# Four gate groups of a hybrid decoder layer as a seven-product block, with its operand sums kept in memory

## The chip, the cores and the metric

The kernel runs on one core of a Trainium2 chip. The metric is the device time of one execution in microseconds (us). The kernel before takes 2213.79 us, the median of 3 runs (2211.71 to 2217.8).

## What is computed

One layer on 1024 tokens with a width of 1024. From the normalised input h come three branches (an mLSTM, a causal differential attention, a cross-attention into 256 memory tokens). Each is projected, multiplied by a sigmoid gate made from h, and summed; an output projection, a residual and an MLP follow. What the change touches is the gate:

```
h     = RMSNorm(x)                                  # 1024 x 1024
gates = sigmoid(h @ w_gate + b_gate)                # 1024 x 3072: 1024 columns for each branch
merged = sum over the branches b of  gates[b] * (y[b] @ w_proj[b])
x = x + merged @ w_out
x = x + relu(RMSNorm(x) @ w_up)**2 @ w_down
```

All of it is float32. TensorE gets each operand as two parts, a rounded high part and the rest (`split`, L104 to L112: ScalarE casts, VectorE subtracts), and a product takes three matmuls, high with high, high with low and low with high (`mm3`).

## The kernel before

`hT` holds h, transposed and split, in SBUF: 8 slices k of 128 features, each with a high and a low part of 1024 tokens. `gate_steps` (L446) is a generator that makes the gates in 12 groups of 256 columns. A group is four products of 128 columns with 512 tokens, and each sums over the 8 slices: 4 x 8 x 3 = 96 matmuls of 128x512. ScalarE takes each product out of PSUM with a tanh (tile `gt`, L471), and SyncE (SP) stores it to `gates` in memory (L472). The 16 weight tiles of 256 KB and their splits (`gate_load`, L431) come two slices at a time.

The order of the work is that of the program text, spread over the engines by a scheduler; where `self.pinned` is set, TensorE's order is that of the text. The table `(2, 1, 1, 2, 6)` cuts the 12 groups into runs: two beside the cross-attention, one and one inside the mLSTM branch, two behind it (the loop at `pg`), and a last run of six, of which three serve as filling inside the attention (until `gdone` is 288) and three follow it (`pgh`).

`branch_d` is the differential attention. Its `d_gemm` (L907) makes 64 tiles of 128 tokens with 384 columns (q, k and v of half a head), 24 matmuls each. A tile is called d tile here. ScalarE copies a d tile's q and k to `draw` (L947), squares them into `dscr` (L949), casts v to `dv` (L111); VectorE sums the squares (L953) and makes the low part of v (L112). Only then is the PSUM bank free. All of these products, gates too, share two banks in turn (`mm_tile`, `kmm` = 2), so a product can start when the last but one has been taken out. Weight tiles `raw` from `in_wd` come by SP and are split into `w` (128x384).

The last instructions of the mLSTM branch are two ScalarE scalings of `ym` (L771), and SP stores each to y (L327). `ym` has one buffer, so the second waits until the first store has landed.

`tail` (L1274) projects and merges. `k_tiles` (L1262) loads a branch's y in 8 tiles `kraw` of 512 KB through two buffers and splits them into `kt`; the first group of 256 columns takes them in that order, 12 matmuls to a tile. The third branch's y comes first.

Of the kernel before, what the change touches and what calls it, by code (L numbers as in the profile page):

```python
# [10 lines left out]
F32 = mybir.dt.float32  # L11
F32R = mybir.dt.float32r
AF = mybir.ActivationFunctionType
# [4 lines left out]
P = 128  # L18
# [3 lines left out]
NK = 8  # L22
# [9 lines left out]
def f32(ap):  # L32
    return ap.bitcast(F32)
# [38 lines left out]
class Layer:  # L72
# [359 lines left out]
    def gate_load(self, pool=None):  # L432

        pool = pool or self.gwp
        n = self.gate_n
        if n == 12 * NK:
            return
# [528 lines left out]
    def branch_d(self, pool):  # L966
# [649 lines left out]
    def run(self):  # L1616
        tc, nc = self.tc, self.nc
        with ExitStack() as ctx:
# [21 lines left out]
            self.rd = dt("r_d", (16, P, 7, 512))  # L1640
            with ExitStack() as c1:
# [6 lines left out]
                with ExitStack() as c2:  # L1648
# [10 lines left out]
                    self.gates = self.gate_steps((2, 1, 1, 2, 6))  # L1659
# [19 lines left out]
                with tc.tile_pool(name="wpg", bufs=13, reuse_waits="tile") as self.wp, tc.tile_pool(name="rpg", bufs=3, reuse_waits="tile") as self.rp:  # L1679
                    self.gwp, self.grp = self.wp, self.rp  # L1680
                    with tc.tile_pool(name="pg", bufs=2) as self.gpool:
                        for _ in range(2 * 32):
                            next(self.gates)
                    cg.close()
                    with tc.tile_pool(name="pd", bufs=2) as pd, tc.tile_pool(name="pd3", bufs=3) as pd3, tc.tile_pool(name="pdm", bufs=1) as pdm, tc.tile_pool(name="pd5", bufs=7) as pd5, tc.tile_pool(name="pdv", bufs=5) as pdv, tc.tile_pool(name="pdv2", bufs=17) as pdv2, tc.tile_pool(name="pd4", bufs=4) as pd4:
# [6 lines left out]
                        class T4:  # L1692
                            def tile(_, shape, dt, tag, name):
                                tag = "dscr2" if tag == "gt" else tag
                                p = pd5 if tag == "draw" else pdv if tag == "drr" else pdv2 if tag == "dv" else pd4 if tag in ("dk", "dkl") else pdm if tag == "dpe1" else pd3 if tag in ("daT", "dst") else pdm if tag in ("dscr", "dscr2", "y", "dsg") else pd
# [12 lines left out]
def pack(i):  # L1708
# [28 lines left out]
    w["wgate"] = np.stack([grp(wg, r(256 * g, 256)) for g in range(12)])  # L1737
# [33 lines left out]
```

## Time and profile before

| | before |
|---|---|
| time, median of 3 runs | 2213.79 us |
| the profiled execution | 2213.57 us, its span 2211.8 us |
| TensorE matmuls busy | 2163.4 us, 98% |
| VectorE, ScalarE, GpSimd busy | 62%, 44%, 24% |
| bytes moved by DMA | 273.06 MB, mean 123 GB/s |

The span is the time between the first and the last recorded instruction, and 1.8 us of the execution lie around it. TensorE is busy nearly all the time, but its ends are modelled, so this says that it rarely waits and not that it runs at its peak. In the rows, PE is TensorE, DVE is VectorE, ACT is ScalarE, POOL is GpSimd, and SPq is the queue of transfers that SP issues. L91 and L94 are the helpers through which every matmul and transpose goes, L111 and L112 the two halves of `split`, so such groups are told apart by their tiles.

### The profile page before, as it was taken

To read this page: it belongs to the slowest core of one execution; us is meant where nothing else is said; L and a number is where in the kernel's file an instruction comes from. 1 tells how busy PE (TensorE), PEld (TensorE's weight loads), DVE (VectorE), ACT (ScalarE), POOL (GpSimd) and SP (SyncE) were. 2 spreads that over 40 slices of the span, in tenths; PEclk is the share of its full clock that TensorE was granted. 3 is DMA by queue.
4 is the path that set the end of the run, shared out by engine and by line. 5 is a ranking of instruction groups with operands and counts; after the bars stand their busy time and mean duration, and the time that the engine had idled before them with its cause. 6 is when DMAs were issued, how large, how long until landed. Compare 5 with 4: busy or idle time off the path is not lost.

```text
span 2211.8 us, 30588 instructions
## 1 busy us (share of the span) xinstructions
PE 2163.4 (98%) x11097; PEld 1860.7 (84%) x11097; DVE 1361.4 (62%) x2598; ACT 980.7 (44%) x1962; POOL 527.8 (24%) x696
## 2 busy tenths in 40 slices
PE   7999999999999999999999999999999999899999
PEld 5878888898899999999888888877787888688887
DVE  6643575565237777777641232544688877767779
ACT  6543355454336666666542120223444444543332
POOL 2100000000011111111000003202557655565553
PEclk9999999999999999999999999999999999999999
DMA  7023122121333333333343443436435444854444
GB/s 250 29 81 115 50 91 76 44 82 39 107 109 86 93 84 84 88 92 86 101 148 114 134 142 126 138 110 205 147 115 198 159 147 147 318 196 146 145 145 170
DMA packets 127948, 273.06 MB, mean 123 GB/s; under 512 B 12945, under 2 KB 21430, under 8 KB 125750
## 3 DMA queue, kind: packets, MB, share of 16 engines
q1 hardware_dynamic: 125494, 258.53, 37.2%
q10 hardware_dynamic: 2304, 12.58, 1.4%
q8 instruction: 87, 1.43, 0.3%
q14 instruction: 63, 0.52, 0.1%
HBM read 178.76 MB, written 67.14 MB: 111 GB/s over the span
## 4 chain that ended last, share of the span: by engine, by line
PE 77%; DVE 9%; DMA 6%; ACT 4%; issue 2%; POOL 2%; SPq 0%; DVEq 0%; ACTq 0%; POOLq 0%
PE mm L91 46%; PE p L91 20%; PE sc L91 6%; PE tp L94 2%; PE po L91 2%; DVE acc L67 1%; DMA kraw<-y 1%; DMA xr<-h_d 1%; DVE wo L67 1%; DMA y<-yd 1%; DVE u L67 1%; DVE w L112 1%; DMA wraw<-in_wup 0%; DVE xts L67 0%; DVE c L67 0%
## 5 line engine op out<-in xcount | busy, mean ns | idle before, releaser
L91 PE MATMUL mm<-w,hT 128*128 128x384 f32 (+3 forms) x2496 | 473.4, 332 | 8.3 <-DVE dsg L112 5.4
L91 PE MATMUL mm<-hT,w 128*128 128x512 f32 x1920 | 465.7, 395 | 0.0
L91 PEld LDWEIGHTS mm<-hT,w 128*128 128x128 f32 x1920 | 353.5, 188 | 74.2
L91 PEld LDWEIGHTS mm<-w,hT 128*128 128x128 f32 x2496 | 389.2, 190 | 22.2 <-DVE dsg L112 7.6
L91 PE MATMUL p<-xd,wo 128*128 128x512 f32 x1344 | 310.0, 393 | 5.7 <-DVE c L67 2.2
L91 PE MATMUL p<-xo,wo 128*128 128x512 f32 x1344 | 308.2, 390 | 5.7 <-DVE st L1418 2.6
L91 PEld LDWEIGHTS p<-xd,wo 128*128 128x128 f32 x1344 | 253.8, 189 | 61.7 <-DVE c L67 3.3
L91 PEld LDWEIGHTS p<-xo,wo 128*128 128x128 f32 x1344 | 251.0, 188 | 61.5 <-DVE u L67 3.7
L91 PE MATMUL mm<-kt,w 128*128 128x512 f32 x1152 | 262.2, 389 | 1.9 <-ACT w L111 1.1
L112 DVE TENSOR_TENSOR w<-raw,w 128x256 fp32r<-128x256 f32 (+3 forms) x304 | 173.0, 590 | 137.9 <-ACT w L111 136.8
L91 PEld LDWEIGHTS mm<-kt,w 128*128 128x128 f32 x1152 | 216.0, 188 | 47.9 <-ACT w L111 1.5
L111 ACT CAST w<-raw 128x256 fp32r<-128x256 f32 (+3 forms) x304 | 154.3, 530 | 178.9 <-PE mm L91 114.5
L104 ACT CAST wo<-wraw 128x896 fp32r<-128x896 f32 x122 | 115.0, 945 | 208.9 <-PE p L91 115.2
L67 DVE TENSOR_TENSOR wo<-wraw,wo 128x896 fp32r<-128x896 f32 x122 | 143.7, 1195 | 59.4 <-ACT wo L104 59.4
L1145 POOL TENSOR_TENSOR wraw<-wraw 128x128 f32<-128x128 f32 x128 | 97.3, 760 | 245.8 <-DMA wraw<-in_wdown 108.1
L1007 ACT ACTIVATE dpe<-sc,dst,drr 128x256 f32<-128x256 f32 (+7 forms) x128 | 106.7, 834 | 99.7 <-DVE dst L1003 92.0
L999 DVE CUSTOM_DVE_ANT_0 sc<-sc,tmask 128x256 f32<-128x256 f32 (+7 forms) x128 | 97.0, 758 | 12.6 <-PE sc L91 12.5
L127 POOL TENSOR_SCALAR hss<-hss 128x4 f32<-128x4 f32 x8 | 3.3, 410 | 415.4 <-ACT mscr L752 272.9
L91 PE MATMUL sc<-dk,dq 128*128 128x512 f32 (+3 forms) x384 | 90.4, 343 | 0.0
L1148 POOL TENSOR_TENSOR wraw<-wraw 128x128 f32<-128x128 f32 x128 | 85.6, 669 | 10.0
L1146 POOL TENSOR_TENSOR wraw<-wraw 128x128 f32<-128x128 f32 x128 | 87.3, 682 | 0.0
L1147 POOL TENSOR_TENSOR wraw<-wraw 128x128 f32<-128x128 f32 x128 | 87.2, 682 | 0.0
(283 smaller groups left out, 2832.6 us busy)
## 6 DMA issues: line engine op xcount, KB each, us to landing
dk<-dsg SPq DMA_DIRECT2D x64, 256.0 KB, 4.4
wraw<-in_wup SPq DMA_DIRECT2D x64, 256.0 KB, 3.4
r_d<-xts SPq DMA_DIRECT2D x16, 1024.0 KB, 4.1
wraw<-in_wdown SPq DMA_DIRECT2D x64, 256.0 KB, 3.1
xd<-r_d SPq DMA_DIRECT2D x19, 768.0 KB, 7.4
xd<-r_d SPq DMA_DIRECT2D x14, 1024.0 KB, 6.8
raw<-in_wgate SPq DMA_DIRECT2D x48, 256.0 KB, 3.2
gates<-gt SPq DMA_DIRECT2D x48, 256.0 KB, 2.0
```

The lines of the kernel that those rows point to most:

```text
L67: return self.tc.keep_in_program_order(f(*a, **k))
L91: self.pin(self.nc.tensor.matmul(out, l, r, start=start, stop=stop))
L94: self.pin(self.nc.tensor.transpose(out, x, self.ident))
L104: self.A.copy(hi, src)
L111: nc.scalar.copy(hi, src)
L112: nc.vector.tensor_sub(lo, src, f32(hi))
L999: V.tensor_tensor_reduce(out=sc[:, 0:n], in0=sc[:, 0:n], in1=self.tmask[:, D - n : D], scale=1.0, scalar=-3.0e38, op0=ALU.add, op1=ALU.max ...
L1007: nc.scalar.activation(pe[c][:, 0:n], sc[:, 0:n], AF.Exp, bias=t8[:, 2 + c : 3 + c], scale=rr[:, i, c : c + 1], accum_out=t8[:, 4 + c : 5 ...
L1145: G.tensor_add(r[:, 4], r[:, 0], r[:, 3])
L1146: G.tensor_sub(r[:, 5], r[:, 4], r[:, 1])
L1147: G.tensor_sub(r[:, 6], r[:, 1], r[:, 0])
L1148: G.tensor_sub(r[:, 7], r[:, 2], r[:, 5])
```

## The change

Groups 8 to 11 are taken out of the generator, which now has runs of (2, 1, 1, 1, 3): one group follows the mLSTM branch where two did, and the attention is filled with three as before. A new function `wino_gates` makes the other four behind the attention. It takes 256 features by 256 columns as a 2 x 2 block of operands, and gets the four quarter products from seven products in place of eight, by the table `PROD`: for each of 4 units (256 columns), 7 products over 4 slice pairs, 3 matmuls each, 84 in place of 96. VectorE and ScalarE add the products up (`u2`, `c11`, `u3`, `c21`). Five of the seven need sums of operands. Those of the weights are made by GpSimd as the tiles come in (32 operations of 128x256). Those of h are four sets of 2 MB; `h_sums` makes them beside the one group that is left behind the mLSTM branch, for each of 4 slice pairs one VectorE addition of 128x2048 (`hb`), three VectorE subtractions and one GpSimd subtraction of 128x512 (`ht`), and a split of 128x2048 (`ho`), stores them to `hc_d`, and `wino_gates` loads four tiles `hx` of 2 MB. In the attention some tiles have pools of their own. The weights of the last four groups are packed as quarters (`wgq`, 256 KB a tile as before).

```diff
--- before.py
+++ after.py
@@ -433,7 +433,7 @@
 
         pool = pool or self.gwp
         n = self.gate_n
-        if n == 12 * NK:
+        if n == 8 * NK:
             return
         g, k = divmod(n, NK)
         if k % 2 == 0:
@@ -1110,9 +1110,112 @@
                 combine(s)
         fill(8)
         norm(15, 2)
-        assert self.gdone <= 288
-        while self.gdone < 288:
+        assert self.gdone <= 256
+        while self.gdone < 256:
             next(gates)
+        self.pinned = False
+
+    def h_sums(self, pool, op):
+
+        nc, V, G = self.nc, self.nc.vector, self.nc.gpsimd
+        for kp in range(4):
+            b = pool.tile([P, 4, 512], F32, tag="hb", name=self.name("hb"))
+            t = pool.tile([P, 4, 512], F32, tag="ht", name=self.name("ht"))
+            o = op.tile([P, 4, 2, 512], F32R, tag="ho", name=self.name("ho"))
+            h = f32(self.hT[:, 2 * kp : 2 * kp + 2])
+            V.tensor_add(b.rearrange("p (k h) n -> p k (h n)", k=2), h[:, :, 0], h[:, :, 1])
+            V.tensor_sub(t[:, 0], b[:, 0], b[:, 1])
+            G.tensor_sub(t[:, 2], b[:, 2], b[:, 0])
+            V.tensor_sub(t[:, 1], b[:, 2], t[:, 0])
+            V.tensor_sub(t[:, 3], b[:, 3], t[:, 1])
+            self.split(o[:, :, 0], o[:, :, 1], t)
+            nc.sync.dma_start(
+                self.hcd[:, :, kp].rearrange("q p n -> p q n"), f32(o).rearrange("p q a n -> p q (a n)")
+            )
+
+    def wino_gates(self, base):
+
+        nc, V, A, G = self.nc, self.nc.vector, self.nc.scalar, self.nc.gpsimd
+        one = lambda name, bufs=1: base.enter_context(tc.tile_pool(name=name, bufs=bufs, reuse_waits="tile"))
+        tc = self.tc
+        gtp, ev, x3, x6, rr, x5, x4 = one("fgt", 2), one("fev", 2), one("fx3"), one("fx6"), one("fr", 3), one("fx5"), one("fx4")
+        X = {}
+        for q, p in ((4, x4), (5, x5), (6, x6), (3, x3)):
+            X[q] = p.tile([P, 4, 2, 512], F32R, tag="x", name=self.name("hx"))
+        raws, W = {}, []
+
+        def load(n):
+            if n < 8:
+                u, kk = divmod(n, 2)
+                r = rr.tile([P, 8, 2, P], F32, tag="fr", name=self.name("fr"))
+                for i in range(2):
+                    nc.sync.dma_start(r[:, 0:4, i], self.a["wgq"][u][:, 2 * kk + i])
+                G.tensor_add(r[:, 4], r[:, 0], r[:, 3])
+                G.tensor_sub(r[:, 5], r[:, 4], r[:, 1])
+                G.tensor_sub(r[:, 6], r[:, 1], r[:, 0])
+                G.tensor_sub(r[:, 7], r[:, 2], r[:, 5])
+                raws[n] = r
+
+        def wsp():
+            n = len(W)
+            if n < 56:
+                u, r = divmod(n, 14)
+                j, kk = divmod(r, 2)
+                t = self.wp.tile([P, 2, 256], F32R, tag="w", name=self.name("w"))
+                self.split(t[:, 0], t[:, 1], raws[2 * u + kk][:, 1 + self.PROD[j][0]].rearrange("p k n -> p (k n)"))
+                W.append(t)
+                if j == 6:
+                    load(2 * u + 3 + kk)
+
+        def x_(q, kp, i):
+            if q >= 3:
+                return X[q][:, kp, i]
+            k, hf = divmod(q + 1, 2)
+            return self.hT[:, 2 * kp + k, i, hf * 512 : hf * 512 + 512]
+
+        for n in range(3):
+            load(n)
+        for q in (4, 5, 6, 3):
+            nc.sync.dma_start(f32(X[q]).rearrange("p k a n -> p k (a n)"), self.hcd[q - 3])
+        for _ in range(9):
+            wsp()
+        self.pinned = True
+        tl = lambda n: ev.tile([P, 512], F32, tag=n, name=self.name(n))
+        for u in range(4):
+            def out(i, c):
+                ft, s = 16 + u * 2 + i // 2, slice(i % 2 * 512, i % 2 * 512 + 512)
+                t = gtp.tile([P, 512], F32, tag="gt", name=self.name("gt"))
+                A.activation(t, c, AF.Tanh, bias=self.bg[:, ft : ft + 1], scale=0.5)
+                nc.sync.dma_start(self.gdr[ft, :, s], t)
+
+            for j, (l, q) in enumerate(self.PROD):
+                ps = self.mm_tile()
+                for kp in range(4):
+                    w = W[u * 14 + 2 * j + kp // 2]
+                    c = slice(kp % 2 * P, kp % 2 * P + P)
+                    self.mm3(ps, (w[:, 0, c], w[:, 1, c]), (x_(q, kp, 0), x_(q, kp, 1)), kp == 0, kp == 3)
+                    if kp % 2:
+                        wsp()
+                if j == 0:
+                    u2, c11, u3, c21 = (tl(n) for n in ("u2", "c11", "u3", "c21"))
+                    A.copy(u2, ps)
+                elif j == 1:
+                    V.tensor_add(c11, u2, ps)
+                    out(1, c11)
+                elif j == 2:
+                    V.tensor_add(u2, u2, ps)
+                elif j == 3:
+                    V.tensor_add(u3, u2, ps)
+                elif j == 4:
+                    V.tensor_add(c21, u3, ps)
+                    out(3, c21)
+                elif j == 5:
+                    V.tensor_add(u3, u3, ps)
+                    V.tensor_add(u2, u2, ps)
+                    out(2, u3)
+                else:
+                    V.tensor_add(u2, u2, ps)
+                    out(0, u2)
@@ -1638,6 +1741,7 @@
             self.x1d = dt("x1_d", (8, P, D))
             self.h2d = dt("h2_d", (8, P, D))
             self.rd = dt("r_d", (16, P, 7, 512))
+            self.hcd = dt("hc_d", (4, P, 4, 1024))
             with ExitStack() as c1:
                 E1 = lambda *x, **k: c1.enter_context(tc.tile_pool(*x, **k))
                 self.pmm = E1(name="pmm", bufs=1, space=PSUM)
@@ -1656,7 +1760,7 @@
                                 p = tmp8 if tag == "xk" else tmp if tag in ("mx", "sq", "r1", "r4") else tmp0
                                 return p.tile(shape, dt, tag=tag, name=name)
                         self.phase_x(kv, T())
-                    self.gates = self.gate_steps((2, 1, 1, 2, 6))
+                    self.gates = self.gate_steps((2, 1, 1, 1, 3))
                     with tc.tile_pool(name="pc", bufs=2) as pc, tc.tile_pool(name="pc1", bufs=1) as pc1, tc.tile_pool(name="pc3", bufs=5) as pc3, tc.tile_pool(name="pc4", bufs=6) as pc4, tc.tile_pool(name="wpc", bufs=8) as self.gwp, tc.tile_pool(name="rpc", bufs=2) as self.grp:
                         class T2:
                             def tile(_, shape, dt, tag, name):
@@ -1678,11 +1782,15 @@
                     self.branch_m(T3(), gm, 1, gnext)
                 with tc.tile_pool(name="wpg", bufs=13, reuse_waits="tile") as self.wp, tc.tile_pool(name="rpg", bufs=3, reuse_waits="tile") as self.rp:
                     self.gwp, self.grp = self.wp, self.rp
-                    with tc.tile_pool(name="pg", bufs=2) as self.gpool:
-                        for _ in range(2 * 32):
+                    with tc.tile_pool(name="pg", bufs=2) as self.gpool, tc.tile_pool(name="phs", bufs=1, side="right", reuse_waits="tile") as phs, tc.tile_pool(name="pho", bufs=2, side="right", reuse_waits="tile") as pho:
+                        self.h_sums(phs, pho)
+                        for _ in range(32):
                             next(self.gates)
                     cg.close()
...
                         self.gpool = T4()
                         self.branch_d(T4())
-                    with tc.tile_pool(name="pgh", bufs=2) as self.gpool:
-                        for _ in self.gates:
-                            pass
+                    with ExitStack() as c3:
+                        self.wino_gates(c3)
             self.tail()
```

On VectorE the end of the mLSTM branch and the start of the attention read so before. `w` are weight splits (`raw` 128x384 for the d tiles), and the last rows take out d tile 0 (`mm_6090`, `dv_6119`) and d tile 1.

```order
L112 TENSOR_TENSOR w_6343<-raw_6280,w_6343 128x384
L112 TENSOR_TENSOR w_6354<-raw_6282,w_6354 128x384
L112 TENSOR_TENSOR w_6363<-raw_6282,w_6363 128x384
L112 TENSOR_TENSOR w_6381<-raw_6284,w_6381 128x384
L953 TENSOR_REDUCE drr_6089<-dscr_6117 128x4
L112 TENSOR_TENSOR dv_6119<-mm_6090,dv_6119 128x128
L953 TENSOR_REDUCE drr_6089<-dscr_6150 128x4
```

And so in the changed kernel, the last of the four sets and the same d tile (`mm_6007`, `dv_6036`):

```order
L112 TENSOR_TENSOR w_6298<-raw_6201,w_6298 128x384
L1126 TENSOR_TENSOR hb_5812<-hT 128x2048
L112 TENSOR_TENSOR ho_5803<-ht_5802,ho_5803 128x4x512
L1127 TENSOR_TENSOR ht_5813<-hb_5812 128x512
L1129 TENSOR_TENSOR ht_5813<-hb_5812,ht_5813 128x512
L1130 TENSOR_TENSOR ht_5813<-hb_5812,ht_5813 128x512
L112 TENSOR_TENSOR ho_5814<-ht_5813,ho_5814 128x4x512
L953 TENSOR_REDUCE drr_6006<-dscr_6034 128x4
L112 TENSOR_TENSOR dv_6036<-mm_6007,dv_6036 128x128
```

All four sets stand ahead of the two VectorE operations that free the bank of d tile 0. From the first `hb`, which stands behind two weight splits, to `dv_6036` there are 4 `hb`, 12 `ht`, 4 `ho`, 11 weight splits, and the last two rows. On ScalarE the cast of the last `ho` stands in the same way ahead of the copy of d tile 0.

At the start of the tail SP issues the loads of the third branch's y (`kraw`) so before; `in_wpc` are weights of the projection, and the weights of the last gate groups are loaded behind these rows:

```order
L472 DMA gates<-gt_12188 128x512
L327 DMA y<-yd_12200 128x512
L1268 DMA kraw_12913<-y 128x1024
L1268 DMA kraw_12918<-y 128x1024
L137 DMA raw_12953<-in_wpc 128x1024
L472 DMA gates<-gt_12265 128x512
```

And so in the changed kernel, where `gt_12915`, `gt_12963`, `gt_12981` and `gt_12998` are the four outputs of the last unit:

```order
L1189 DMA gates<-gt_12915 128x512
L137 DMA raw_13283<-in_wpc 128x1024
L1371 DMA kraw_13117<-y 128x1024
L1189 DMA gates<-gt_12963 128x512
L1371 DMA kraw_13122<-y 128x1024
L1189 DMA gates<-gt_12981 128x512
L1408 DMA gl_13267<-gates 128x512
L1408 DMA gl_13271<-gates 128x512
L1189 DMA gates<-gt_12998 128x512
L1371 DMA kraw_13127<-y 128x1024
```

The first load of y has moved from the start of the last three groups to the last unit of the block: its buffer takes memory of the operand tile `hx` that the fifth product of a unit reads, and it waits for that product's last matmul in the fourth unit, two products (24 matmuls) before the end of the block. The second load stands behind the store of the output `gt_12963`, and the third behind that of the last output.

## Rows read from the trace of the kernel before

**Rows 1.** The page, first lines: span, and TensorE's busy time.

```profile
span 2211.8 us, 30588 instructions
PE 2163.4 (98%) x11097; PEld 1860.7 (84%) x11097; DVE 1361.4 (62%) x2598; ACT 980.7 (44%) x1962; POOL 527.8 (24%) x696
```

**Rows 2.** TensorE's waits: line and tile, releaser, us in total, times, longest.

```profile
PE mm L91 <- DVE dsg L112: 5.4, 7, 0.9
...
PE mm L91 <- DVE w L112: 3.8, 3, 3.0
```

**Rows 3.** Timeline, gates and tail: start, us, engine, line, out<-in, xcount [idle before].

```profile
1151.72 66.94 PE L91 MATMUL mm<-hT,w 128*128 128x512 f32 x294
1218.50 43.68 PE L91 MATMUL mm<-kt,w 128*128 128x512 f32 x192
```

**Rows 4.** Timeline, end of the mLSTM branch, two groups, first d tiles.

```profile
575.53 44.40 PE L91 MATMUL mm<-hT,w 128*128 128x512 f32 x192
576.10 0.73 ACT L771 ACTIVATE ym<-tho,dv 128x512 f32<-128x512 f32 x1 [0.42 <-DVE tho L768]
...
576.93 0.40 SPq L327 DMA_DIRECT2D y<-ym  x1
...
615.76 3.28 DVE L112 TENSOR_TENSOR w<-raw,w 128x384 fp32r<-128x384 f32 x5 [24.00 <-ACT w L111]
...
619.77 19.43 PE L91 MATMUL mm<-w,hT 128*128 128x384 f32 x111
```

**Rows 5.** Tiles `xts` and `xo` (MLP operands): ns min/median/max, first and last start.

```profile
L1127 DVE TENSOR_TENSOR xts<-xr x4: 692/693/962, 1523.4 to 1593.0; 128x512 f32<-128x512 f32 x4
L1128 POOL TENSOR_TENSOR xts<-xr x4: 1383/1742/1797, 1523.5 to 1591.2; 128x512 f32<-128x512 f32 x4
L1129 DVE TENSOR_TENSOR xts<-xr,xts x4: 680/1667/1672, 1524.1 to 1594.3; 128x512 f32<-128x512 f32 x4
...
L111 ACT CAST xo<-xts x4: 1891/1916/1919, 1526.6 to 1596.3; 128x2048 fp32r<-128x2048 f32 x4
L112 DVE TENSOR_TENSOR xo<-xts,xo x4: 2278/2429/2586, 1528.7 to 1599.1; 128x2048 fp32r<-128x2048 f32 x4
```

**Rows 6.** Groups by line and shape: busy us, mean ns, then idle before.

```profile
L112 DVE TENSOR_TENSOR w<-raw,w 128x384 fp32r<-128x384 f32 x64 | 34.6, 554 | 32.4 <-ACT w L111 31.4
...
L953 DVE TENSOR_REDUCE drr<-dscr 128x4 f32<-128x256 f32 x64 | 26.5, 415 | 30.0 <-ACT dscr L949 30.0
...
L112 DVE TENSOR_TENSOR dv<-mm,dv 128x128 fp32r<-128x128 f32 x64 | 18.1, 283 | 0.1
```

**Rows 7.** DMA issues: tensors, count, KB each, median us to landing.

```profile
r_d<-xts SPq DMA_DIRECT2D x16, 1024.0 KB, 4.1
...
kraw<-y SPq DMA_DIRECT2D x24, 512.0 KB, 4.5
...
y<-ym SPq DMA_DIRECT2D x16, 256.0 KB, 2.0
```

**Rows 8.** Timeline of TensorE around its waits behind `w`, `st`.

```profile
1533.26 1.22 PE L91 MATMUL mm<-mh,w 128*128 128x512 f32 x2 [3.00 <-DVE w L112]
...
1589.32 7.05 PE L91 MATMUL p<-xo,wo 128*128 128x512 f32 x30 [2.62 <-DVE st L1418]
```

**Rows 9.** Stretches: us, busy by engine, then granted TensorE clock, DMA share, GB/s.

```profile
202.00:208.00 6.00, 5.27 (x21) 4.89 (x22) 2.83 (x8) 3.08 (x9) 0.00 (x0) 0.50 0.42 132
...
1533.00:1536.00 3.00, 2.74 (x7) 2.17 (x8) 2.42 (x2) 0.00 (x0) 1.33 (x1) 0.50 0.80 181
...
1589.00:1592.00 3.00, 2.68 (x12) 2.27 (x13) 1.86 (x4) 3.00 (x6) 2.65 (x3) 1.00 0.32 93
```

**Rows 10.** Tile `kraw` (ns min/median/max), then us from issue to landing.

```profile
L111 ACT CAST kt<-kraw x24: 1047/1052/1057, 1160.5 to 1409.7; 128x1024 fp32r<-128x1024 f32 x24
L112 DVE TENSOR_TENSOR kt<-kraw,kt x24: 1210/1225/1433, 1161.6 to 1410.7; 128x1024 fp32r<-128x1024 f32 x24
...
DMA to landing us min/median/max: 3.2/4.5/6.7
```

More of the change, by code (lines that the diff above doesn't have):

```diff
@@ L1680, in run @@
                     self.gwp, self.grp = self.wp, self.rp
-                    with tc.tile_pool(name="pg", bufs=2) as self.gpool:
-                        for _ in range(2 * 32):
+                    with tc.tile_pool(name="pg", bufs=2) as self.gpool, tc.tile_pool(name="phs", bufs=1, side="right", reuse_waits="tile") as phs, tc.tile_pool(name="pho", bufs=2, side="right", reuse_waits="tile") as pho:
+                        self.h_sums(phs, pho)
+                        for _ in range(32):
                             next(self.gates)
                     cg.close()
-                    with tc.tile_pool(name="pd", bufs=2) as pd, tc.tile_pool(name="pd3", bufs=3) as pd3, tc.tile_pool(name="pdm", bufs=1) as pdm, tc.tile_pool(name="pd5", bufs=7) as pd5, tc.tile_pool(name="pdv", bufs=5) as pdv, tc.tile_pool(name="pdv2", bufs=17) as pdv2, tc.tile_pool(name="pd4", bufs=4) as pd4:
+                    with ExitStack() as c3:
+                        E3 = lambda name, bufs: c3.enter_context(tc.tile_pool(name=name, bufs=bufs, reuse_waits="tile"))
+                        pdo, pdy, pdv2, pdm, pds, pd5 = E3("pdo", 2), E3("pdy", 1), E3("pdv2", 17), E3("pdm", 1), E3("pds", 1), E3("pd5", 7)
+                        pdv, pd, pd3, pd4 = E3("pdv", 5), E3("pd", 2), E3("pd3", 3), E3("pd4", 4)
                         self.tmask = pdm.tile([P, D], F32, name="tmask")
@@ L1694, in tile @@
                                 tag = "dscr2" if tag == "gt" else tag
-                                p = pd5 if tag == "draw" else pdv if tag == "drr" else pdv2 if tag == "dv" else pd4 if tag in ("dk", "dkl") else pdm if tag == "dpe1" else pd3 if tag in ("daT", "dst") else pdm if tag in ("dscr", "dscr2", "y", "dsg") else pd
+                                p = {
+                                    "draw": pd5, "drr": pdv, "dv": pdv2, "dk": pd4, "dpe1": pdm, "daT": pd3, "dst": pd3,
+                                    "dscr": pds, "dsg": pds, "dscr2": pdy, "y": pdy, "doS": pdo, "dso": pdo,
+                                }.get(tag, pd)
                                 return p.tile(shape, dt, tag=tag, name=name)
@@ L1698, in run @@
                         self.branch_d(T4())
-                    with tc.tile_pool(name="pgh", bufs=2) as self.gpool:
-                        for _ in self.gates:
-                            pass
+                    with ExitStack() as c3:
+                        self.wino_gates(c3)
             self.tail()
@@ L1736, in pack @@
     wg = i["w_gate"][0]
-    w["wgate"] = np.stack([grp(wg, r(256 * g, 256)) for g in range(12)])
+    w["wgate"] = np.stack([grp(wg, r(256 * g, 256)) for g in range(8)])
+    w["wgq"] = quads(wg[:, 2048:])
     for n, s in (("wpm", "w_proj_m"), ("wpd", "w_proj_d"), ("wpc", "w_proj_c"), ("wout", "w_out")):
```

## The prediction, made before the changed kernel was run

> **What bounds the kernel now.** I read the page's busy times first: matmuls fill 2163.4 of a span of 2211.8 us [rows 1]. The list of TensorE's waits comes next; the largest inside the attention is 5.4 us in seven pieces, and that for a weight split `w` is 3.8 in three [rows 2]. So a matmul taken away is worth its own time wherever no other wait steps in, and a wait put in costs its full length. Then the timeline gives the rate of a gate matmul: 294 of them from 1151.72 to the tail's first at 1218.50, without a wait: 66.78 / 294 = 0.227 us each [rows 3]. Last I read the stretch where the new work is put. Two gate groups run from 575.53 to 619.77, 22.1 us each, and then the d tiles, 24 matmuls in 19.43 / 111 x 24 = 4.2 us [rows 4].
>
> The sums below are made against the profiled execution, 2213.6 us (2211.8 of span and 1.8 around it); it lies 0.2 below the median of the runs.
>
> **Matmuls removed.** Four groups of 96 become four units of 84, so 48 fall away: 48 x 0.227 = **-10.9 us**. Within a unit a product takes 12 x 0.227 = 2.7 us. VectorE has per product two weight splits and at most two sums, each no longer than the 0.69 us of a 128x512 subtraction [rows 5]: at most 2.8 us, and mostly less. With two banks TensorE doesn't wait: 0.
>
> **The sums of h.** This is work that the kernel before doesn't have, and it is put ahead of d tile 0's release on VectorE. The nearest rows are the same operations in the MLP, on equal shapes [rows 5]. The addition `hb` and the low half of `ho` go by the 128x2048 row: 2.278 at least, 2.429 in the median. A subtraction takes 0.692, the last cast on ScalarE 1.92. With the other rows of the queue [rows 6] the chain from the first `hb` to `dv` of d tile 0 is:
>
> - 4 `hb` and 4 low halves: 8 x 2.278 = 18.2
> - 12 subtractions: 12 x 0.692 = 8.3
> - 11 weight splits: 11 x 0.554 = 6.1
> - the squares' sum and `dv`: 0.415 + 0.283 = 0.7
> - the last cast, which nothing on VectorE covers: 1.9
> - GpSimd's subtraction beside VectorE, four times: the L1129 row has 1.667 where GpSimd works and 0.680 where it doesn't, so 4 x 0.98 = 3.9
>
> Together 39.1 us. The Trainium skill ("SBUF — State Buffer", section "SBUF: two separate sides") calls the port pair shared by VectorE and GpSimd an exclusive lock that blocks the loser for a whole instruction. By that rule and the 1.742 of the GpSimd row the last line would be 7.0 and not 3.9, and the sum 3.1 us worse; the row shows the smaller loss, and the forecast goes by the row.
>
> When does the chain start? The first `hb` waits for the last `ym`, and that for the landing of the store before it: 576.93 + 2.0 [rows 4, 7] + 0.73 = 579.7. So `dv` of d tile 0 is done at 579.7 + 39.1 = 618.8. TensorE comes to the third d tile after one group and two d tiles: 575.5 + 22.1 + 8.4 = 606.0. That tile needs the bank of the first. The stall is **+12.8 us**. Without the GpSimd line it is 8.9. With 2.429 for the long operations it is 14.0, and 2 more if the squares' sum has to wait for the store of the third set (a 2 MB store lands in about 4.1 + 2.1 x 1024 / 768 = 6.9 us by the rows of 256 and 1024 KB [rows 7], which is an estimate; behind it VectorE still has 7 us to do): 16.0. Below nothing it can't be, as the group's 22.1 us and two d tiles are all the cover there is, 26.3 us from the chain's start. With two groups, as before, the cover would be 48 us and the stall nothing.
>
> Queued behind the chain are d tile 0 and all later ones on VectorE, and on SP behind the four stores of 2 MB the next head's weights and `dq`, which are wanted many d tiles later: 0.
>
> **The clock behind the stall.** After 3.00 us of idle TensorE [rows 8] the granted clock read 0.50, the lower of the two levels (1.2 of 2.4 GHz), for the 3 us from 1533; from 202 to 208 it read 0.50 for 6 us [rows 9]. After an idle of 2.62 us it stayed 1.00 [rows 8, 9]. The stall is longer than each, so I count one such stretch: half of 3 to half of 6 us lost, taken at **+2.3**, at least 0.
>
> **Operands of the block.** `hx` is 4 x 2 MB and the weights are 256 KB tiles as before. They are issued under the last group that fills the attention; its 22 us and the 5.4 us of the first two products, which read h itself, cover the first set of 6.9. Cost 0; if that cover is gone, about 6.
>
> **The start of the tail.** Before, the first y tiles came in under the three groups, and the tail began without a wait [rows 3]. Now the first load is issued 24 matmuls (5.4 us) before the block's end, and two buffers go round: 0.3 to issue, 4.5 to land, 1.05 to cast, 1.23 for the low half [rows 10], 7.1 us for two tiles. TensorE uses up two in 24 x 0.227 = 5.4. The third load stands behind the store of the last output, some 2.6 us after the end, so tile 3 is ready at 9.7, tile 5 at 16.8, tile 7 at 23.9. In the changed order 90 matmuls, 20.4 us, stand ahead of tile 7's low half: **+3.5 us**. With the shortest landing, 3.2, tile 7 is in time and only a start of 0.5 is left; with the longest, 6.7, it is 10. I take the median.
>
> **Sum.** -10.9 + 12.8 + 2.3 + 3.5 = +7.7: 2213.6 + 7.7 = **2221.3 us**. Its own ends: -10.9 + 8.9 + 0 + 0.5 = -1.5, 2212.1; and -10.9 + 16.0 + 3.0 + 10 = +18.1, 2231.7.
>
> **Rivals.**
> - *The sums are hidden, and the kernel is faster.* If `dv` of d tile 0 is done by 606.0, the stall and the clock fall away: 2213.6 - 10.9 + 3.5 = 2206.2, and 2203.2 with a tail that starts after 0.5. For it: VectorE stood idle for 24.00 us in one piece in that stretch [rows 4]. Against it: it decides at a chain of 26.3 us, and the long operations and subtractions alone are 26.5 by their shortest rows. Chance 0.13.
> - *The block waits for its operands.* Each `hx` of 6.9 us serves a product of 2.7, so if their loads start late, the third to sixth products of the first unit wait: some 6 us more, 2227.3. For it: the loads stand in one queue with the gates' stores and weights. Against it: 27 us of cover. Chance 0.10.
> - *The block doesn't save what it says.* With two banks and chains of sums on VectorE, a wait of 0.3 us in each of 28 products would give back 8.4 us: 2229.7. Against it: each product gives VectorE 2.7 us, and two banks let one be late. Chance 0.07.
> - The forecast has the rest, 0.70.
>
> **How the numbers follow.** A measurement of this kernel tells about 0.3% (6.6 us) from no change, so "same" is 2207.2 to 2220.4. The forecast lies just above; of its 0.70 I put 0.40 above the bound and 0.29 inside, with 0.01 for a stall still smaller. The two costly rivals add 0.16 to slower and 0.01 to same, the first gives 0.13 to faster. So faster 0.14, same 0.30, slower 0.56. The range takes in the forecast's ends but for the last us, and reaches down to part of the first rival: 2207 to 2231.
>
> **What would show it.** Right: one wait of TensorE at line 91 for `dv` (L112), 9 to 16 us long, at the third d tile; a granted clock of 0.50 behind it for some us; VectorE busy without a break from about 580 to 618; 336 matmuls of the block in about 76 us; waits for `kt` of 1 to 10 us in sum at the start of the tail. Wrong: no wait for `dv` over 5 us (the first rival), waits for `hx` (the second), or many short waits inside the block (the third).

## The result and the profile after

The changed kernel takes 2225.05 us in the median of 7 runs (2217.31 to 2228.04), the kernel before 2213.79 beside it (7 runs, 2211.55 to 2217.8). The ratio is 1.0044, with a 95% interval of 1.0032 to 1.0056: slower by 7 to 12 us. The forecast was 2221.3 in a range of 2207 to 2231, with the larger chance on slower.

The profiled execution took 2227.09 us, 2.0 more than the median. The first lines of its page, to be held against [rows 1]:

```profile
span 2225.2 us, 30692 instructions
...
PE 2161.3 (97%) x11049; PEld 1856.9 (83%) x11049; DVE 1425.6 (64%) x2670; ACT 999.1 (45%) x1994; POOL 560.6 (25%) x732
```

There are 48 matmuls fewer, but TensorE's busy time fell by 2.1 us only, not by 10.9, in part because some of the matmuls that are left ran at the lower clock; and the span is 13.4 longer. TensorE's waits in the changed kernel (line and tile, releaser, us in total, times, longest) hold two of over 3 us that were not in the list of before:

```profile
PE mm L91 <- DVE dv L112: 11.3, 1, 11.3
...
PE mm L91 <- DVE dsg L112: 5.6, 7, 0.9
...
PE mm L91 <- ACT u L1201: 3.3, 1, 3.3
...
PE mm L91 <- DVE dsg L115: 1.6, 1, 1.6
```

The wait for `dsg` at L112 is the one of before [rows 2]. The wait for `dv` is the forecast's stall. The wait for `u`, the first sum of the block, is a term that the forecast had at nothing. Where they lie shows in TensorE's timeline (start, us, engine, line, out<-in, xcount [idle before]), whose rows answer to [rows 4] and [rows 3]:

```profile
575.86 22.64 PE L91 MATMUL mm<-hT,w 128*128 128x512 f32 x96
598.35 8.51 PE L91 MATMUL mm<-w,hT 128*128 128x384 f32 x48
618.16 12.99 PE L91 MATMUL mm<-w,hT 128*128 128x384 f32 x63 [11.31 <-DVE dv L112]
...
1146.12 7.15 PE L91 MATMUL mm<-hT,w 128*128 128x512 f32 x30
1156.60 12.78 PE L91 MATMUL mm<-hx,w 128*128 128x512 f32 x48 [3.32 <-ACT u L1201]
1169.22 8.32 PE L91 MATMUL mm<-hT,w 128*128 128x512 f32 x36
1177.38 11.04 PE L91 MATMUL mm<-hx,w 128*128 128x512 f32 x48
1188.26 8.32 PE L91 MATMUL mm<-hT,w 128*128 128x512 f32 x36
...
1230.00 7.52 PE L91 MATMUL mm<-kt,w 128*128 128x512 f32 x32 [0.78 <-POOL ones L1416]
```

TensorE comes to the third d tile after the one group and 48 matmuls, as the forecast has it, and stands 11.3 us. The 63 matmuls behind it take 12.8 us from start to start (618.16 to the next row at 630.99), and at [rows 4]' rate of 0.175 they would take 11.0. At the start of the block 48 matmuls on `hx` take 1169.22 - 1156.60 = 12.6 us, while in the second unit the same 48 take 10.9. The stretches (us, busy of PE, PEld, DVE, ACT, POOL, granted clock, DMA share, GB/s) say why:

```profile
619.00:622.00 3.00, 3.00 (x11) 3.00 (x10) 0.00 (x0) 0.00 (x0) 0.00 (x0) 0.50 1.02 407
622.00:625.00 3.00, 3.00 (x19) 3.00 (x18) 0.00 (x0) 0.57 (x3) 0.00 (x0) 0.98 1.00 305
...
1157.00:1158.00 1.00, 1.00 (x6) 0.83 (x5) 0.99 (x2) 0.70 (x1) 0.92 (x3) 1.00 0.04 11
1158.00:1160.00 2.00, 2.00 (x7) 1.51 (x6) 0.72 (x1) 0.43 (x2) 2.00 (x3) 0.50 0.34 131
1160.00:1161.00 1.00, 1.00 (x4) 0.81 (x3) 0.05 (x1) 0.00 (x0) 0.92 (x3) 0.50 0.00 0
1161.00:1165.00 4.00, 4.00 (x18) 3.27 (x18) 2.42 (x5) 1.22 (x3) 0.64 (x1) 0.95 0.00 0
```

Behind both waits the granted clock reads 0.50, 1.2 of 2.4 GHz, for about 3 us. Behind the shorter one the engine first ran at 1.00 again, and the clock fell afterwards.

The two traces side by side, by five points that both have:

| stretch | before | after | difference |
|---|---|---|---|
| start to the last transposes of the mLSTM | 574.7 | 575.1 | +0.3 |
| from there to the attention's first scores | 78.1 | 70.1 | -8.0 |
| to the attention's last transposes | 498.6 | 500.6 | +2.1 |
| to the tail's first matmul | 67.1 | 84.2 | +17.1 |
| the tail | 993.3 | 995.2 | +1.9 |

In the second row a group of 22.1 us went away, and 11.3 of stall and 1.8 of clock came in (-9.0; 1.0 is left over). In the fourth the group came back in another form: 22.1 less the 10.9 of the matmuls is 11.2, and 3.3 of wait, 1.7 of clock and 0.8 ahead of the tail's first matmul make 17.0.

**The stall.** VectorE's timeline, from the first `hb` to `dv` of d tile 0:

```profile
580.49 2.29 DVE L1126 TENSOR_TENSOR hb<-hT 128x2048 f32<-128x2048 f32 x1 [1.87 <-ACT ym L771]
...
583.16 1.79 DVE L1127 TENSOR_TENSOR ht<-hb 128x512 f32<-128x512 f32 x1
...
592.36 0.68 DVE L1127 TENSOR_TENSOR ht<-hb 128x512 f32<-128x512 f32 x1
...
596.84 2.29 DVE L1126 TENSOR_TENSOR hb<-hT 128x2048 f32<-128x2048 f32 x1 [1.19 <-POOL ht L1128]
...
615.29 2.29 DVE L112 TENSOR_TENSOR ho<-ht,ho 128x2048 fp32r<-128x2048 f32 x1 [2.01 <-ACT ho L111]
617.50 0.41 DVE L953 TENSOR_REDUCE drr<-dscr 128x4 f32<-128x256 f32 x1
617.83 0.28 DVE L112 TENSOR_TENSOR dv<-mm,dv 128x128 fp32r<-128x128 f32 x1
```

From 580.49 to 618.11 the chain stops only twice, in the 1.19 and 2.01 us that the rows give, and it is 37.6 us long; the forecast had 39.1, from 579.7. The rows explain the difference: an operation mostly starts some 0.08 us before the end that the row of the one ahead shows (592.36 + 0.68 is 593.04, and the next starts at 592.96), which over the 33 operations makes 2.1 us; about half a microsecond goes the other way, most of it beside GpSimd. GpSimd's four subtractions stand beside it:

```profile
582.93 1.48 POOL L1128 TENSOR_TENSOR ht<-hb 128x512 f32<-128x512 f32 x1 [14.86 <-DVE hb L1126]
592.05 4.76 POOL L1128 TENSOR_TENSOR ht<-hb 128x512 f32<-128x512 f32 x1 [7.64 <-DVE ho L112]
```

**The start of the block.** ScalarE's timeline shows what the copy `u` stood behind, and SyncE's queue (second fence) what that waited for:

```profile
1155.35 0.40 ACT L111 CAST w<-fr 128x256 fp32r<-128x256 f32 x1 [4.40 <-DMA fr<-in_wgq]
1155.96 0.58 ACT L1201 COPY u<-mm 128x512 f32<-128x512 f32 x1 [0.20 <-DMA gates<-gt]
```

```profile
1150.86 0.94 SPq L1152 DMA_DIRECT2D fr<-in_wgq  x2
1151.89 0.45 SPq L472 DMA_DIRECT2D gates<-gt  x1
```

Ahead of `u` stands a cast of a weight tile of the second unit. That tile's load was issued at 1150.86, when one of the three `fr` buffers came free, and ScalarE stood 4.40 us for it. Behind it the copy waits 0.20 more for the store of the attention's last gate output, issued at 1151.89: the tile of `u` lies where that output lay. Two banks go round, so the third product waits for the copy.

### The profile page after: what moved, and what is told of

Same layout as the page of the kernel before. It is cut to its first block, busy times and chain, and to the rows that moved or that the text cites. A ratio compares the mean times of both kernels' runs of the same rounds, so it can differ in the third digit from the quotient of the medians.

```text
span 2225.2 us, 30692 instructions
## 1 busy us (share of the span) xinstructions
PE 2161.3 (97%) x11049; PEld 1856.9 (83%) x11049; DVE 1425.6 (64%) x2670; ACT 999.1 (45%) x1994; POOL 560.6 (25%) x732
## 4 chain that ended last, share of the span: by engine, by line
PE 73%; DVE 11%; DMA 7%; ACT 4%; issue 3%; POOL 2%; SPq 0%; DVEq 0%; ACTq 0%; POOLq 0%
PE mm L91 41%; PE p L91 20%; PE sc L91 6%; PE tp L94 2%; PE po L91 2%; DVE w L112 1%; DMA kraw<-y 1%; DVE acc L67 1%; DMA xr<-h_d 1%; DVE wo L67 1%; DVE u L67 1%; ACT dpe L1007 1%; ACT w L111 1%; DVE xts L67 0%; DVE c L67 0%
## 5 line engine op out<-in xcount | busy, mean ns | idle before, releaser
L91 PE MATMUL mm<-w,hT 128*128 128x384 f32 (+3 forms) x2496 | 475.9, 333 | 21.0 <-DVE dv L112 11.3
L91 PEld LDWEIGHTS mm<-w,hT 128*128 128x128 f32 x2496 | 391.7, 191 | 35.2 <-DVE dv L112 11.6
L91 PE MATMUL mm<-hT,w 128*128 128x512 f32 x1680 | 412.0, 396 | 0.0
L91 PEld LDWEIGHTS mm<-hT,w 128*128 128x128 f32 x1680 | 308.4, 188 | 64.9
L111 ACT CAST w<-raw 128x256 fp32r<-128x256 f32 (+3 forms) x272 | 142.0, 545 | 151.7 <-PE mm L91 124.0
L112 DVE TENSOR_TENSOR w<-raw,w 128x256 fp32r<-128x256 f32 (+3 forms) x272 | 160.2, 607 | 70.8 <-ACT w L111 70.0
L999 DVE CUSTOM_DVE_ANT_0 sc<-sc,tmask 128x256 f32<-128x256 f32 (+7 forms) x128 | 96.9, 757 | 12.5 <-PE sc L91 12.4
```

The lines of the kernel that those rows point to most:

```text
L91: self.pin(self.nc.tensor.matmul(out, l, r, start=start, stop=stop))
L111: nc.scalar.copy(hi, src)
L112: nc.vector.tensor_sub(lo, src, f32(hi))
L999: V.tensor_tensor_reduce(out=sc[:, 0:n], in0=sc[:, 0:n], in1=self.tmask[:, D - n : D], scale=1.0, scalar=-3.0e38, op0=ALU.add, op1=ALU.max ...
```

## Experiments

All are compared with the kernel before; its median in the three sessions was 2214.88 (experiments 1 to 4), 2215.05 (5 to 8) and 2212.96 us (9 and 10). The changed kernel itself was not run again in them, so a difference to its 2225.05 is rough by some 2 us.

**1. The sums taken out.** Is the stall the sums' chain on VectorE, and what is it worth?

```diff
 for kp in range(4):
     ...
-    V.tensor_add(b.rearrange(...), h[:, :, 0], h[:, :, 1])
-    V.tensor_sub(t[:, 0], b[:, 0], b[:, 1])
-    G.tensor_sub(t[:, 2], b[:, 2], b[:, 0])
-    V.tensor_sub(t[:, 1], b[:, 2], t[:, 0])
-    V.tensor_sub(t[:, 3], b[:, 3], t[:, 1])
-    self.split(o[:, :, 0], o[:, :, 1], t)
-    nc.sync.dma_start(self.hcd[:, :, kp]..., f32(o)...)
+    nc.sync.dma_start(self.hcd[:, :, kp]..., h...)
```

> The changed kernel with the sums left out: h itself is stored to memory in their place, as many bytes in four stores of 2 MB, and read back as before (so the last four gate groups get other operands). Theory (the sums' chain on VectorE holds the bank of the first d tile): the wait for dv of 11.3 us goes, the half clock behind it (2.0) too, and 1 to 2 us of later waits in the attention; 2225 - 14 = about 2211, with the block's own wait of 3.3 us at its third product unchanged. Rival (the added transfers slow what runs beside them, and the chain only looks long): a wait of several us stays at the same place, 2220 or more.

Measured: 2209.47 us, ratio 0.9979 (0.997 to 0.9987). The wait for `dv` is gone; TensorE's timeline goes from the gate group through the d tiles without a break, as in [rows 4]:

```profile
596.53 19.43 PE L91 MATMUL mm<-w,hT 128*128 128x384 f32 x111
```

By the medians the sums cost 2225.05 - 2209.47 = 15.6 us, by the spans of the two profiled executions 12.6; stall and clock are 13.1 in the rows above and 15.1 in the forecast. The wait for `u` is still there (3.1 us), so it has another cause.

**2. The copy ahead of the casts.** Is the wait at the start of the block a matter of ScalarE's order?

```diff
-self.split(t[:, 0], t[:, 1], r)
+cast = A.copy(t[:, 0], r)
+if u and j == 0:
+    tc.add_manual_dep(cast.ins, copies[-1].ins.name, no, reason="order")
+V.tensor_sub(t[:, 1], r, f32(t[:, 0]))
...
-A.copy(u2, ps)
+copies.append(A.copy(u2, ps))
```

> The changed kernel with one order fixed: in each unit ScalarE takes the first product out of its bank before it casts the first two weight tiles of the next unit. Theory (ScalarE's copy of the first product stood behind a cast whose weights had only been issued 4 us before): the wait of 3.3 us at the block's third product goes, and the half clock behind it, 1.9: 2225 - 5.2 = about 2220. Rival (the third product waits for its operand tile, which lands at that time anyway): TensorE waits as long for hx, 2225.

Measured: 2222.68 us, ratio 1.004 (1.0026 to 1.0054), less gained than expected. The wait is 2.3 us in place of 3.3, and the 48 matmuls behind it took 11.0 us, so the clock didn't fall there. Neither can be put down to the edit: in the runs that leave this order as it was (experiments 1, 3, 5, 9 and 10) the wait is 1.5 to 3.1 us. ScalarE's timeline shows the copy, now ahead of the cast, waiting for the store alone:

```profile
1154.31 0.58 ACT L1206 COPY u<-mm 128x512 f32<-128x512 f32 x1 [4.70 <-DMA gates<-gt]
```

Two things held the copy, then: the order, and the store whose memory it reuses. In the changed kernel the second stood only 0.20 us behind the first, so taking away the order alone left nearly the whole wait.

**3. The first load of the tail earlier.** Does it matter where the first `kraw` load takes its memory? The operand tiles of the third and the fifth product change places (`x4` and `x6` in the code).

```diff
-gtp, ev, x3, x6, rr, x5, x4 = one("fgt", 2), one("fev", 2), one("fx3"), one("fx6"), ...
+gtp, ev, x3, x4, rr, x5, x6 = one("fgt", 2), one("fev", 2), one("fx3"), one("fx4"), ...
```

> The changed kernel with two operand tiles exchanged in memory, so that the first load of y takes the memory of the tile that the third product reads, not the fifth: it can be issued 48 matmuls before the block's end, not 24. Theory (the tail starts late because its first loads are issued late): waits for kt of 1.4 us at the tail's start go, and up to 2.7 us in all: 2222.4 to 2224. Rival (the round of two buffers sets the pace, so an earlier first load helps the first tiles alone): 2225, with the waits moved to later tiles.

Measured: 2225.11 us, ratio 1.0044 (1.0031 to 1.0057): the same as the change itself. The load was issued 5.8 us earlier (1218.15 in place of 1223.90) and the tail began without a wait, but TensorE waits for weights instead, 5.6 us where it was 3.7 (and 3.8 in [rows 2]):

```profile
PE mm L91 <- DVE w L112: 5.6, 3, 3.0
```

**4. Half of the sums earlier.** Sets 2 and 3 are made inside the mLSTM branch in 8 pieces of 128 columns, together with the edits of experiments 2 and 3. The planner places them; their operations on VectorE are not held to the written order.

```diff
+for i, (kp, c) in enumerate((kp, c) for kp in (2, 3) for c in range(4)):
+    add(110 + 40 * i, self.h_piece, self.hpp, kp, c)
...
-self.h_sums(phs, pho)
+self.h_sums(phs, pho, (0, 1))
```

> The changed kernel with the two edits of the runs before it and with half of the sums moved: the sets of the last two slice pairs are made in eight pieces of 128 columns spread over the mLSTM branch, the other two sets beside the gate group as now. Everything is computed. Theory: the chain ahead of the first d tile falls to about 20 us and is covered, the block's wait and the tail's go, and what is left is the 48 matmuls: 2213.8 - 10.9 + 0 to 3 = 2203 to 2206, faster than both kernels. Rival (VectorE has no room in the mLSTM branch either, 17 us of pieces show up there as waits of TensorE): 2210 or more.

Measured: 2215.35 us, ratio 1.0004 (0.9996 to 1.0013). The wait for `dv` is gone, as expected, but the mLSTM ends 10.5 us later than before (585.23 in place of 574.74), with new waits in it:

```profile
PE tp L91 <- DVE g_col L566: 3.6, 1, 3.6
...
PE tp L526 <- DVE g_two L521: 2.9, 1, 2.9
```

All eight pieces ran between 198.7 and 257.9 us, ahead of and among the small operations of the mLSTM's gates, which TensorE waits for (`g_two` at 248.8 us in place of 243.5, `g_col` at 269.4 in place of 258.9). That is the stall once more, on the same engine, in another place.

**5. Three sets, the third stored twice.** Does the stall shrink with the chain?

```diff
-for kp in range(4):
+for kp in range(3):
     ...
+    if kp == 2:
+        nc.sync.dma_start(self.hcd[:, :, 3]..., f32(o)...)
```

> The changed kernel with three of the four sets of sums made; the third is stored twice in place of the fourth (so the last four gate groups get other operands), so the bytes stored stay. Theory (the chain's length on VectorE less its cover): one set is 2.3 + 2.3 + 2.1 us of VectorE and 1 of GpSimd beside it, and the last cast still shows, so the wait for dv falls from 11.3 to 2.5 to 4, and the clock stays at 1.00 behind it or falls for a short stretch: 9 to 11 us less, about 2215. Rival (any chain that ends in a store and a cast costs about the same): the wait stays near 11, 2225.

Measured: 2229.51 us, ratio 1.0067 (1.0054 to 1.008): slower still, with a wait of 16.5 us for `dv`. The expectation failed. (The profiled execution is the fastest of the five, 2223.78 us.) VectorE's chain ended early, at 609.3, and then:

```profile
607.00 2.29 DVE L112 TENSOR_TENSOR ho<-ht,ho 128x2048 fp32r<-128x2048 f32 x1 [1.55 <-ACT ho L111]
622.17 0.42 DVE L953 TENSOR_REDUCE drr<-dscr 128x4 f32<-128x256 f32 x1 [12.88 <-DMA hc_d<-ho]
```

The sum of squares `drr` of d tile 0 is written where an `ho` tile lay, and waits until that tile's store has landed. Here two stores of 2 MB stood one behind the other, issued at 609.3 and 609.7, and VectorE went on 12.4 us after the second.

**6. Both causes of the block's wait removed.** Experiment 2, and the sums' pool placed ahead of the gate outputs' pool, so that `u` lies in other memory.

```diff
-gtp, ev, x3, x6, ... = one("fgt", 2), one("fev", 2), ...
+ev, gtp, x3, x6, ... = one("fev", 2), one("fgt", 2), ...
```

> The changed kernel with ScalarE's copy of a unit's first product ahead of the next unit's casts, as in the run before, and with the pool of the sums u2, c11, u3, c21 placed ahead of that of the outputs, so that u2 no longer takes the memory of the attention's last gate output. Theory (the copy waited for two things at once: the late weight tile, and the store of that output, which stands behind the weights' load on SP): with both gone the wait at the block's third product falls from 3.3 to under 0.5 and the clock stays at 1.00: 5 us less, 2220. Rival (the operand tiles land no earlier, and TensorE waits for hx): 2 us less as with the first edit alone, the rest under another name.

Measured: 2221.36 us, ratio 1.0031 (1.002 to 1.0041). The copy runs as soon as its product is done, and TensorE goes on through the third and the fourth product before it waits 0.56 us:

```profile
1150.44 0.59 ACT L1206 COPY u<-mm 128x512 f32<-128x512 f32 x1 [0.21 <-PE mm L91]
```

```profile
1152.96 5.60 PE L91 MATMUL mm<-hx,w 128*128 128x512 f32 x24
1159.12 5.75 PE L91 MATMUL mm<-hx,w 128*128 128x512 f32 x24 [0.56 <-DVE u L1211]
```

By the medians 3.7 us came back of the 5.0 of wait and clock, and TensorE waits nowhere for `hx`.

**7. The block alone.** The edits of experiments 1 and 6 together: what are seven products in place of eight worth, without either wait?

> The kernel that stores h in place of the sums (so the last four gate groups get other operands), with the two edits of the run before. Theory: nothing is left then but the 48 matmuls less and the tail's start: 10.9 - 2 to 3 = 8 to 9 us faster than before, 2205 to 2207, and the waits of TensorE those of the kernel before but for kt. Rival (the block itself runs slower than its count, by evacuations or clock): within 5 us of before.

Measured: 2204.59 us, ratio 0.9954 (0.9942 to 0.9966), which is 10.2 us below before; the 48 matmuls were put at 10.9. This kernel leaves out the sums of h, so the 10.2 us are what the block alone is worth.

**8. Everything computed, the sums spread and held in place.** Experiment 4, but the pieces start later, their VectorE operations are held to the written order, and the sums' pool lies as in experiment 6.

```diff
-    add(110 + 40 * i, self.h_piece, self.hpp, kp, c)
+    add(150 + 50 * i, self.h_piece, self.hpp, kp, c)
...
-    V = self.nc.vector
+    V = self.V
...
-    self.split(o[:, :, 0], o[:, :, 1], b)
+    self.split2(o[:, :, 0], o[:, :, 1], b)
...
-gtp, ev, x3, x4, ... = one("fgt", 2), one("fev", 2), ...
+ev, gtp, x3, x4, ... = one("fev", 2), one("fgt", 2), ...
```

> The combined kernel with the pieces of the sums pinned in VectorE's order behind the mLSTM branch's gates (they stood ahead of them, and TensorE waited 7 us there) and the sums' pool ahead of the outputs'. Everything is computed. Theory: the 10 us that the combined kernel lost in the mLSTM branch come back but for 1 to 3, and the block's wait is gone: 2204 to 2208, faster than both kernels. Rival (VectorE's 17 us are paid wherever they are put in that branch): 2212 or more.

Measured: 2206.48 us (2202.82 to 2213.98), ratio 0.9963 (0.9948 to 0.9977): 0.2 to 0.5% faster than the kernel before, and faster than the changed one. The rows to compare are the same two stretches of TensorE's timeline, and the tail's first matmul:

```profile
577.15 1.03 PE L94 MATMUL tp<-ident,hS 128*128 128x128 f32 x8
...
600.40 19.43 PE L91 MATMUL mm<-w,hT 128*128 128x384 f32 x111
...
1143.20 11.44 PE L91 MATMUL mm<-hx,w 128*128 128x512 f32 x48
...
1214.39 8.55 PE L91 MATMUL mm<-kt,w 128*128 128x512 f32 x37
```

The pieces make the mLSTM 2.4 us longer, not 10.5, the d tiles don't wait, and the block starts without a wait. TensorE comes to the tail at 1214.39, where it was 1218.50 before [rows 3] and 1230.00 in the change. Three things differ from experiment 4 (the later start, the held order, the place of the pool), and they were not tried singly; the pool bears on the wait for `u`, which was 1.5 us in experiment 4.

**9. Three sets again, the last one stored once.** Was it the store, in experiment 5, that took the chain's place? Now the first set is stored twice, and the last store stands alone.

```diff
-    if kp == 2:
+    if kp == 0:
         nc.sync.dma_start(self.hcd[:, :, 3]..., f32(o)...)
```

> Three sets of sums again, but now the first set is the one stored twice in place of the fourth (so the last four gate groups get other operands), and the third is stored once. Theory formed on the run before it (the first d tile's sum of squares lies in memory of the third set, so VectorE also waits until that store has landed): VectorE is done with the third set near 609.3 as before, one store of 2 MB lands 7 to 8 us later, so dv is done near 617.5 and the wait of TensorE is 10 to 12 us, as long as with all four sets; about 2223 to 2225. Rival (the chain's length alone counts, and the last run's 16.5 us was the doubled store): the wait falls to 2.5 to 4, about 2215.

Measured: 2220.63 us, ratio 1.0027 (1.0017 to 1.0037), with a wait of 10.2 us for `dv`: the wait that was expected, in a time 2.4 us below what was expected (the profiled execution took 2223.87).

```profile
607.80 2.29 DVE L112 TENSOR_TENSOR ho<-ht,ho 128x2048 fp32r<-128x2048 f32 x1 [2.02 <-ACT ho L111]
616.82 0.42 DVE L953 TENSOR_REDUCE drr<-dscr 128x4 f32<-128x256 f32 x1 [6.73 <-DMA hc_d<-ho]
```

The chain is 7.5 us shorter than in the change (its last row starts at 607.80, there at 615.29), and the sum of squares starts only 0.7 earlier. It was the store. In the change itself the third store had landed by 616.90 (the copy of d tile 1 waits for it until then) and the chain ended at 617.50: two limits, 0.6 us apart.

**10. GpSimd's subtraction on VectorE.** What do the two engines cost each other?

```diff
-G.tensor_sub(t[:, 2], b[:, 2], b[:, 0])
+V.tensor_sub(t[:, 2], b[:, 2], b[:, 0])
```

> The changed kernel with GpSimd's subtraction in each set moved to VectorE. Theory (VectorE and GpSimd block each other: in the changed kernel three VectorE subtractions took 1.6 to 1.8 us in place of 0.68, and GpSimd's second one 4.8): four more subtractions cost 2.8 us and give back 4.3, so the chain and the wait for dv get 1 to 2 us shorter, 2223 to 2224. Rival (the work of GpSimd is free beside VectorE): the wait gets 2.8 us longer, 2228.

Measured: 2218.54 us, ratio 1.0022 (1.001 to 1.0034). VectorE has four operations more, and the wait for `dv` is 2.6 us shorter, 8.7. The moved operation (ns min, median, max) and `dv`'s chain:

```profile
L1128 DVE TENSOR_TENSOR ht<-hb x4: 676/680/682, 582.5 to 607.2; 128x512 f32<-128x512 f32 x4
```

```profile
613.61 0.42 DVE L953 TENSOR_REDUCE drr<-dscr 128x4 f32<-128x256 f32 x1
```

Four subtractions of 0.60 from start to start are 2.4 us; the chain that takes them in is 2.6 us shorter all the same, so GpSimd's help cost about 5 us. The time fell by more than the wait did and came out below what was expected; where the rest lies is open.

## Why the prediction was right, step by step

- **Matmuls removed, -10.9: right.** From one unit to the next it is 1196.42 - 1177.38 = 19.04 us where a group by the rate of [rows 3] takes 96 x 0.227 = 21.8. Four of them give -11.0, and experiment 7 gives -10.2 for the whole kernel. Inside the later units TensorE doesn't wait, so the third rival (0.3 us in each product) is out. The step's "With two banks TensorE doesn't wait" counted VectorE alone; in the first unit it was ScalarE that held a bank (below).
- **The stall, +12.8: right in place and cause, 1.5 too large.** It measured 11.3. The chain began 0.8 us later than forecast (580.49 for 579.7) and was 1.5 shorter, for the overlap of neighbouring operations, so it ended 0.7 earlier; and TensorE came to the third d tile 0.8 later (606.85 for 606.0). Experiment 1 takes the chain away and the stall goes with it.
- **What ends the stall: half seen.** The prediction had the wait for the third set's store as an upper end, "2 more"; that doesn't follow from its own numbers (a landing after 6.9 us, with 7 us of work left on VectorE), which put the two limits side by side. So the runs show them: the store had landed 0.6 us before the chain was done. The first rival was to decide "at a chain of 26.3 us"; experiments 5 and 9 show that a shorter chain alone would not have decided it, since `drr` has to wait for a landing in any case. That holds for the memory as it is laid out here. The prediction looked at that store only for the long chain.
- **The clock, +2.3: right**, 1.8 by the rows. With the stall that is 13.1 against 15.1, and experiment 1 has 12.6 to 15.6 for both and what hangs on them.
- **GpSimd beside VectorE, 3.9 in the chain: right in size.** Three subtractions lost 1.1, 1.1 and 1.0 us (1.79, 1.78 and 1.63 against 0.68), and one `hb` waited 1.19 for GpSimd: 4.3 in sum. The price was taken from the row's average, and the rule that the prediction set beside it would have made it 7.0. The manner, though, is the rule's: where GpSimd came first (582.93), VectorE's subtraction ended only after it; where VectorE came first with one two-input operation after another (592.05), GpSimd took 4.76 us in place of 1.48, and VectorE then waited for it. That agrees with the Trainium skill ("SBUF — State Buffer", section "SBUF: two separate sides"), by which the loser is blocked for the whole instruction.
- **Operands of the block, 0: this step failed.** It measured 3.3 of wait and 1.7 of clock, 5.0 us. The step asked whether `hx` and the first weights are there in time, and they were: no wait for `hx` is in the list, so the second rival is out as it was put, though its size of 6 was, by luck, about right. What was late was the copy of the first product. It stood on ScalarE behind a cast of the *next* unit's weights, which waited for a load and that for a buffer; and behind this, a store held its memory. Experiments 2 and 6 take away first the one and then both.
- **The start of the tail, +3.5: right in mechanism, too large.** It measured 2.4. The first matmul starts 0.8 late; the list names `ones` for it, but that was written by 1229.48, and what ended last, at 1229.90, is ScalarE's cast of the first `kt`:

```profile
1228.87 1.03 ACT L111 CAST kt<-kraw 128x1024 fp32r<-128x1024 f32 x1
1229.28 0.20 POOL L1416 MEMSET ones<- 128x128 f32 x1 [28.61 <-PE mm L91]
...
1238.09 107.28 PE L91 MATMUL mm<-kt,w 128*128 128x512 f32 x469 [0.57 <-ACT kt L111]
```

  In experiment 3, where `kt` is early, the first matmul starts at 1228.83, ahead of `ones` at 1229.06. From 1230.00 to 1345.37 there are 501 matmuls, 115.4 us, where the 0.227 of [rows 3] makes 113.7: another 1.6, and 0.6 of it is the second wait for `kt`. The waits for `kt` are so 1.4 us, within the 1 to 10 that were to show it. The same load issued earlier (experiment 3) took them away, but a wait for `w` grew and the time stayed.
- **The rest of the tail** is no measure of the change. Up to the MLP it gives 2.5 us back in shorter waits, and then it loses 2.8 where the MLP's first products run at the lower clock in two stretches, from 1595 and from 1602. The first of them, in the kernel before and after, and the clock after:

```profile
1583.00 3.71 PE L91 MATMUL p<-xo,wo 128*128 128x512 f32 x15
...
1594.41 5.29 PE L91 MATMUL p<-xo,wo 128*128 128x512 f32 x15
...
1595.00:1598.00 3.00, 3.00 (x9) 2.32 (x8) 1.41 (x1) 0.70 (x1) 2.92 (x4) 0.50 0.80 233
```

  From the first `kt` matmul to the end the ten experiments take 990.0 to 996.7 us, with the same work in all, so the 1.9 of the table lies within what one execution differs from another.
- **Left out:** 2.1 us more inside the attention, of which 1.1 are a longer wait for `dsg` at L115 (1.6, before 0.5). That wait is 1.5 to 2.1 us in all ten experiments, and the table's third row 500.7 to 502.7, also where no sums are made (1 and 7), so neither the sums nor the stall is the cause; what the change does there besides, new pools in the attention, was not tried by itself.

The terms as measured are -11.0 + 11.3 + 1.8 + 5.0 + 2.4 + 2.1 = +11.6 of the 13.4 us between the two profiled executions. The forecast's sum was +7.7. The part that was missed is the block's first product, and the stall, the clock and the tail, all put a little too large, hid some of it: that the sum came as near as it did is in part luck. The other 1.8 us are in pieces of 1 us and less, by the table above.

## What to carry to other kernels

A side job put on an engine that works its queue in order costs what it delays behind it, not its own length: list what stands ahead of each operation that frees a bank or a buffer, on every engine that does so (here VectorE's `dv` and ScalarE's copy of a first product), and look at casts for work further on that wait for loads. Count a second limit behind the first: a tile that reuses the memory of one whose store is under way waits for the landing, and shortening the chain ahead of it by 7.5 us shortened the wait by 1.1 here. What gained here was half of the work cut into pieces, put where its engine has room, and held in its place; the same pieces placed earlier and without a fixed order gave the gain back.

## What the runs showed of the hardware

- One GpSimd subtraction of 128x512 took 1.48 us against a single VectorE operation, and 4.76 beside an unbroken run of them. In each of the four sets it ended 1.1 to 1.2 us after the end of a VectorE operation that it had run beside (for the two rows shown, those that end at 583.24 and 595.64), however long it took in all. Moving all four to VectorE, which was the bound there, made the wait of TensorE 2.6 us shorter.
- The eight transfers of 2 MB in the change (four stores and the four loads of `hx`) landed in 6.6 us at the least, 7.8 in the median and 12.8 at most; the estimate was 6.9.
- The length of an idle does not tell by itself whether TensorE's clock falls. After 3.3 us the granted clock still read 1.00 for the first microsecond or more and then 0.50 for about 3 us; after 2.3 us (experiment 2) it stayed at 1.00; after 2.1 us at the same place (experiment 10) it read 0.50, and the 48 matmuls took 12.6 us:

```profile
1151.48 12.75 PE L91 MATMUL mm<-hx,w 128*128 128x512 f32 x48 [2.09 <-ACT u L1201]
...
1152.00:1154.00 2.00, 2.00 (x6) 1.54 (x5) 0.83 (x2) 0.72 (x1) 1.92 (x3) 0.50 0.11 43
```
